# Moving small products, loads and waits in a one-core encoder layer

## The chip, the cores and the metric

The kernel runs on one core of a Trainium2 chip. The metric is the device time of one execution in microseconds (us), the median over several runs. The engines named below are TensorE (PE, matmuls; PEld is its weight load), VectorE (DVE), ScalarE (ACT), GpSimd (POOL) and SyncE (SP). SP, ACT and POOL also issue DMAs, each from a queue of its own that is worked off in order.

## The reference, cut to what matters

One layer of an encoder with a residual stream `h` of 256 tokens by 2048 channels: a hybrid mixer (a gated linear recurrence and an RWKV7 recurrence), cross attention over 256 memory tokens, and a SwiGLU block. Each is followed by a layer norm.

```python
def step(S, inp):                       # RWKV7, 32 heads of 64
    r_t, w_t, k_t, v_t, kk_t, b_t = inp
    sa = jnp.einsum('bhvk,bhk->bhv', S, kk_t)
    S = S * w_t[:, :, None, :] - sa[..., None] * b_t[:, :, None, :] + v_t[..., None] * k_t[:, :, None, :]
    return S, jnp.einsum('bhvk,bhk->bhv', S, r_t)
...
o = group_norm(o) * gn_g + gn_b
o = o + jnp.sum(r_h * k_h * r_k, axis=-1, keepdims=True) * v_h      # the "bonus"
return o * g                                                       # g = sigmoid(g_lo) @ gB
...
s = jnp.einsum('bthd,bmhd->bhtm', q, k) * (XATTN_HEAD_DIM ** -0.5)  # 4 heads of 512
p = jax.nn.softmax(s, axis=-1)
o = jnp.einsum('bhtm,bmhd->bthd', p, v)
h = layer_norm(ALPHA * h + o @ wo)
ff = (jax.nn.silu(h @ wg) * (h @ wu)) @ wd
```

All values are float32. Every large product is made from a high and a low part of both factors.

## The kernel before, in words

**The main stream.** All weights flow through one stream. A weight tile (2048 by 128, 1 MB) comes in two halves of 512 KB. For each half, `split_half` loads `raw` (four buffers, issued by SP), casts it to the high part `wh` on ACT (L156) and subtracts to get the low part `wl` on DVE (L158), three buffers each. In the mixer, `wstat_half` then multiplies: eight matmuls of 512 columns (L169: `wh` times high and low part of the activations) and eight of 256 columns (L172: `wl` times the high part). In the later stages, `xstat` keeps the activations stationary: for each half unit and each of the two token halves (`tt`) six matmuls of 512 columns (L243, L244, L246). `xstat` can group units: it makes all units of a group for token half 0, then all of them for token half 1, and holds a group's weights in tiles that a function `room` gives.

**Deferred work.** Small products run beside the stream. `defer(n, fn)` files a function, and `passed(mm)`, called at the end of every half unit, counts it down. When it is due, its instructions are traced with an order edge: those for PE come behind that matmul `mm`. Only PE is bound by this edge. The order on each engine is otherwise fixed when the program is built, by a planner that takes instructions by priority once they are ready by its own estimate of times. Instructions of the stream carry low priority numbers by their unit, all others count up in the order of tracing. On the chip each engine runs its fixed list in order and waits where data are late.

**The RWKV part.** Sixteen channel tiles form four groups. For each tile, `tile_stage` multiplies key, receptance and value columns (six halves) and defers: `key_direction` (normalized keys, L572 is its matmul), `receptance` (`rkf`, L603), `values` (two transposes L608 copied to `sv` on ACT at L610 and L611, and the bonus product L613 that DVE turns into `yb` at L614), `key_rows` (four transposes L619, copied to `bkt` on ACT at L620) and `products` (L627, masked into `gt` on DVE at L631). The PSUM tiles of all these come from one pool, `mix`, of three banks. `sq`, `rkf` and a group's later `on` share one SBUF buffer (tag A).

Three halves after a group's last tile, `recurrence` starts a triangular solve: SP writes parts of `gt` to DRAM and reads them back as `al`, DVE runs 31 dependent steps (L674, L677), SP writes the result out (L680) and reads it back as `ymat` (L685). PACE halves later `chunk_steps` is traced: DVE transposes `ymat` into `xz` (L692), PE starts with L697 and L707, and four chunks of matmuls follow (L726 to L756), then a group norm. At its end, for each of four tiles, come two transposes (L783), the norm's scale on ACT (L785), the bonus (L786), two products with gate weights `lwg` (L790) loaded on POOL's queue (L457), and the gate (L791). The next group's small work needs buffers that `chunk_steps` still reads, so most of it runs once `chunk_steps` is through. `decay_rates` for the next group loads `lw` and makes L518.

**Attention.** For each of four heads come four tiles of q (eight halves), the scores (L990 to L992), the softmax (L994 to L1001), the transposes of the weights (L1006) and the products with the values (L1014 to L1016) into `oT`. Then `wo` runs in four column blocks. Between blocks, DVE applies the scale and shift of the layer norm before (L1040, L1041) with row broadcasts `gb1` that POOL loads (L1025). The last block has its eight half units in two groups, whose split weights lie in the buffers of the values (`vh0`, `vh1`, `vl0`, `vl1`) and of `B`. Then the first half units of the gate matrix are split ahead into tiles `wsp` (L207, L208), and the second layer norm runs per token half (L926, L328, transposes L336, L338 to L346), queued on ACT and DVE behind these splits.

Of the kernel before, what the change touches and what calls it, by code (L numbers as in the profile page):

```python
# [18 lines left out]
P = 128  # L19
T = 256  # L20
# [7 lines left out]
NT = 16  # L28
NG = 4
DR = (7, 10)  # L30
PACE = (20, 28, 20, 20)
NB0, NB1 = 4, 7
ALPHA = float(2.0 ** 0.25)
LN_EPS = 1e-5
# [11 lines left out]
def trunk(ctx, tc, x, memT, vec, rows, consts, lruw, loraw, w_in, w_out, wq, wk, wv, wo, wgu, wd, out,  # L46
# [31 lines left out]
    def defer(n, fn):  # L78
        waiting.append([n, fn])
# [302 lines left out]
    with ExitStack() as mx:  # L382
# [72 lines left out]
        def small_load(dst, src):  # L455
            with tc.issue_after(front[-1]):
                nc.gpsimd.dma_start(dst, src)  # L457
# [49 lines left out]
        def decay_rates(g, jp, rates):  # L507

            if jp == 0:
                rates.append(grp.tile([P, 4, T], F32, name="avg"))  # L510
                rates.append(grp.tile([P, 4, T], F32, name="evg"))
            avg, evg = rates
            lw = wk1.tile([P, 2, 2, P], F32, name="lw")
            small_load(lw, loraw[2 * g + jp, :, 0:2])
            for n, dst in ((0, evg), (1, avg)):
                ps = mps()
                for jj in range(2):
                    nc.tensor.matmul(ps[:, jj * T:(jj + 1) * T], lw[:, n, jj, :], lo[n], start=True, stop=True)  # L518
                nc.scalar.activation(dst[:, 2 * jp:2 * jp + 2], ps.rearrange("p (j t) -> p j t", j=2), AF.Sigmoid)
            for j in range(2 * jp, 2 * jp + 2):  # L520
                nc.vector.tensor_tensor_scan(evg[:, j], cmask, evg[:, j], 0.0, ALU.mult, ALU.add)
# [40 lines left out]
        def tile_stage(g, j, i, u, fs, av, ev, dt, kr, bkt, sv, yb, gt):  # L562
# [72 lines left out]
            for nm, n in (("k", 1), ("r", 0), ("v", 2)):  # L635
# [4 lines left out]
                    defer(2, key_direction)  # L640
                elif nm == "r":
                    defer(1, receptance)
            defer(1, values)
            defer(2, key_rows)
            defer(3 if j == 3 else 4, products)

        def recurrence(g, kkr, gt, bkt, sv, dm, yb, scr, scx, pace):

# [38 lines left out]
            defer(pace, partial(chunk_steps, g, kkr, gt, bkt, sv, dm, yb, gi))  # L687

        def chunk_steps(g, kkr, gt, bkt, sv, dm, yb, gi):
            for pr in range(2):  # L690
                q = 64 * (1 - pr)
                nc.vector.transpose(xz[q:q + 32], ymat[q:q + 32, :, 0:32])  # L692
# [67 lines left out]
            for a in range(2):  # L760
# [12 lines left out]
                nc.vector.reciprocal(rv, vr)  # L773
                nc.vector.tensor_tensor(o3, o3, rv.rearrange("p (h o) -> p h o", o=1).broadcast_to([P, 8, 64]),
                                        ALU.mult)
            for j in range(4):
                i = 4 * g + j
                fs = slice(j * P, (j + 1) * P)
                lw = wk1.tile([P, 2, P], F32, name="lwg", bufs=2)
                small_load(lw, loraw[i // 2, :, 2:4, i % 2])  # L780
                ps = rps()
                for a in range(2):
                    last = nc.tensor.transpose(ps[:, a * P:(a + 1) * P], ot[a][:, fs], ident)  # L783
                on = wk1.tile([P, T], F32, name="on", tag="A")
                nc.scalar.activation(on, ps[:, 0:T], AF.Identity, scale=col("gn_g", i), bias=col("gn_b", i))  # L785
                nc.vector.tensor_tensor(on, on, yb[:, j, :], ALU.add)  # L786
                ps = rps()
                with tc.issue_after(last.ins):
                    for a in range(2):
                        nc.tensor.matmul(ps[:, 0:T], lw[:, a, :], lo[2 + a], start=(a == 0), stop=(a == 1))  # L790
                nc.vector.tensor_tensor(yb[:, j, :], on, ps[:, 0:T], ALU.mult)  # L791
            dump(f"yb{g}", yb)

        evac = [None]
# [138 lines left out]
    with at:  # L933
# [40 lines left out]
        for hd in range(XH):  # L974
            b0 = 4 * (hd % 2)
            qs = [pair(ap1, "q", f"B{b0 + k}") for k in range(4)]
            qh, ql = [h for h, _ in qs], [l for _, l in qs]
            for k in range(4):
                a = wtile(wq[hd * 4 + k], xTh, xTl)
                split_to(a, qh[k], ql[k])  # L980
            pp = [pair(ap1, "pT", f"B{8 + b0 // 2 + m}") for m in range(2)]
            pTh, pTl = [h for h, _ in pp], [l for _, l in pp]
            pn = []
            for tt in range(2):
                ts = slice(tt * P, (tt + 1) * P)
                ps = mp.tile([P, 512], F32, name="mix", tag="mix")
                s = ps[:, 0:NMEM]
                for k in range(4):
                    kk = hd * 4 + k
                    nc.tensor.matmul(s, qh[k][:, ts], kTh[kk], start=(k == 0), stop=False)  # L990
                    nc.tensor.matmul(s, qh[k][:, ts], kTl[kk], start=False, stop=False)
                    nc.tensor.matmul(s, ql[k][:, ts], kTh[kk], start=False, stop=(k == 3))  # L992
                mxx = sm_.tile([P, 1], F32, name="mxx")
                nc.vector.tensor_reduce(mxx, s, AX.X, ALU.max)  # L994
                pe = ap1.tile([P, NMEM], F32, name="pe", tag=f"B{12 + b0 // 2 + tt}")
                nc.vector.tensor_scalar(pe, s, mxx, None, ALU.subtract)
                sme = sm_.tile([P, 1], F32, name="sme")
                last = nc.scalar.activation(pe, pe, AF.Exp, scale=sc, accum_out=sme)
                rse = sm_.tile([P, 1], F32, name="rse")
                nc.vector.reciprocal(rse, sme)  # L1000
                nc.vector.tensor_scalar(pe, pe, rse, None, ALU.mult)  # L1001
                pn.append(pe)
            for m in range(2):
                ps = mp.tile([P, 512], F32, name="mix", tag="mix")
                for tt in range(2):
                    nc.tensor.transpose(ps[:, tt * P:(tt + 1) * P], pn[tt][:, m * P:(m + 1) * P], ident)  # L1006
                split_to(ps[:, 0:T], pTh[m], pTl[m])
            for k in range(4):
                kk = hd * 4 + k
                cs = slice(kk * P, (kk + 1) * P)  # L1010
                ps = mp.tile([P, 512], F32, name="mix", tag="mix")
                o = ps[:, 0:T]
                for m in range(2):
                    nc.tensor.matmul(o, vh[m][:, cs], pTh[m], start=(m == 0), stop=False)  # L1014
                    nc.tensor.matmul(o, vh[m][:, cs], pTl[m], start=False, stop=False)
                    nc.tensor.matmul(o, vl[m][:, cs], pTh[m], start=False, stop=(m == 1))  # L1016
                oTh[kk], oTl[kk] = pair(ap1, "oT", f"A{kk}")
                split_to(o, oTh[kk], oTl[kk])
        with tc.issue_after(last.ins):
            load_sqrt(sm_)  # L1020
        gb1 = []
# [11 lines left out]
            return [t[:, n * 512:(n + 1) * 512] for n in range(4)]  # L1033

        for nb in range(4):
            pt = xstat([wo[nb, u] for u in range(4)], oTh, oTl, [(4, room), (4, lambda i: room(i + 4))] if nb == 3 else None)
            for m in range(2 * nb, min(2 * nb + 2, 4)):
                for tt in range(2):
                    s = hres[:, tt, m * 512:(m + 1) * 512]
                    nc.vector.tensor_tensor(s, s, gb1[m], ALU.mult)  # L1040
                    nc.vector.tensor_tensor(s, s, gb1[4 + m], ALU.add)  # L1041
            if nb < 3:
                residual(nb, pt, st)
# [194 lines left out]
```

## Time and profile before

| | |
|---|---|
| three runs, median (lowest to highest) | 2109.88 us (2102.26 to 2113.18) |
| profiled execution, its own time | 2105.15 us |
| its span, first to last instruction | 2103.4 us |
| PE busy | 2067.1 us (98%) |
| DVE busy | 1389.2 us (66%) |
| ACT busy | 1097.6 us (52%) |
| mean granted PE clock | 0.993 |

The span and the times inside it come from the one profiled execution. Busy time of PE is modelled from pipelined matmuls, so "busy" can hide a slower pace. A row of the timeline gives start, duration, engine, line, operation, output and inputs, how often, and in brackets the idle time of that engine before it with what ended it.

### The profile page before, as it was taken

The page shows a single profiled execution, that of the slowest core. Times are in us where ns is not written, and L with a number is a line of the kernel's source. Part 1 is how long each engine was busy: PE and PEld are TensorE (multiplying, and loading weights), DVE is VectorE, ACT ScalarE, POOL GpSimd, SP SyncE. Part 2 cuts the span into 40 slices and gives each one's busy share as a digit, 9 for nine tenths or more (in the row PEclk, how much of TensorE's full clock was granted, in tenths as well). Part 3 has the DMA queues.
Part 4 walks back from the last instruction along what each step waited for, and adds up shares of the span by engine and source line. Part 5 has one row for each costly group of instructions (what it writes and reads, how often), then busy time and mean ns, then how long its engine had stood idle before and what let it go on. Part 6 is the DMA issues. An engine that isn't in the chain of part 4 may idle for free.

```text
span 2103.4 us, 30286 instructions
## 1 busy us (share of the span) xinstructions
PE 2067.1 (98%) x11588; PEld 1749.3 (83%) x11588; DVE 1389.2 (66%) x2157; ACT 1097.6 (52%) x1588; POOL 113.5 (5%) x176
## 2 busy tenths in 40 slices
PE   9999999999999999999999999999999999999997
PEld 8888888888888888888888888778888888888886
DVE  7787868968795986686755666645555544444455
ACT  6756755665564575665644444544444444433332
POOL 2100020020002000300000000000000000000000
PEclk9999999999999999999999999999999999999999
DMA  9645635644553465477555455655555555555554
GB/s 327 200 157 180 201 104 161 202 147 145 178 187 116 141 196 179 150 266 239 183 191 197 141 180 175 219 186 190 190 190 190 191 186 193 190 187 195 191 196 143
DMA packets 135761, 388.18 MB, mean 185 GB/s; under 512 B 38368, under 2 KB 42976, under 8 KB 134848
## 3 DMA queue, kind: packets, MB, share of 16 engines
q1 hardware_dynamic: 126368, 358.71, 52.4%
q0 software_dynamic: 6000, 19.27, 2.8%
q10 hardware_dynamic: 3248, 8.26, 1.1%
q8 instruction: 91, 1.49, 0.3%
q14 instruction: 54, 0.44, 0.1%
HBM read 375.31 MB, written 10.88 MB: 184 GB/s over the span
## 4 chain that ended last, share of the span: by engine, by line
PE 62%; DVE 4%; DMA 2%; issue 1%; ACT 1%; POOL 0%; DVEq 0%; SPq 0%; POOLq 0%; ACTq 0%
PE acc L244 15%; PE acc L243 15%; PE acc L246 15%; PE acc L169 7%; PE acc L172 4%; DVE wl L158 1%; DMA kr<-k_d 1%; DMA gb<-in_rows_dram 0%; PE mix L1092 0%; PE rec L731 0%; PE rec L738 0%; PE rec L756 0%; DVE pd L674 0%; DVE xi L677 0%; DMA lwg<-in_loraw_dram 0%
## 5 line engine op out<-in xcount | busy, mean ns | idle before, releaser
L158 DVE TENSOR_TENSOR wl<-raw,wh 128x1024 fp32r<-128x1024 f32 x640 | 782.1, 1223 | 564.9 <-ACT wh L156 522.1
L156 ACT CAST wh<-raw 128x1024 fp32r<-128x1024 f32 x640 | 670.6, 1050 | 673.5 <-PE acc L244 495.2
L169 PE MATMUL acc<-xT,wh 128*128 128x512 f32 x2112 | 556.1, 401 | 0.0
L169 PEld LDWEIGHTS acc<-xT,wh 128*128 128x128 f32 x2112 | 381.3, 190 | 69.0
L172 PEld LDWEIGHTS acc<-xT,wl 128*128 128x128 f32 x2112 | 290.6, 190 | 22.0
L172 PE MATMUL acc<-xT,wl 128*128 128x256 f32 x2112 | 305.6, 285 | 0.0
L243 PE MATMUL acc<-wh,xT 128*128 128x512 f32 x688 | 268.8, 391 | 0.0
L244 PE MATMUL acc<-wh,xT 128*128 128x512 f32 x688 | 267.8, 389 | 0.0
L246 PE MATMUL acc<-wl,xT 128*128 128x512 f32 x688 | 211.9, 389 | 0.4 <-DVE wl L158 0.4
L246 PEld LDWEIGHTS acc<-wl,xT 128*128 128x128 f32 x688 | 129.1, 188 | 27.8 <-DVE wl L158 0.8
L243 PEld LDWEIGHTS acc<-wh,xT 128*128 128x128 f32 x688 | 129.2, 188 | 26.7 <-ACT wh L156 0.2
L244 PEld LDWEIGHTS acc<-wh,xT 128*128 128x128 f32 x688 | 129.2, 188 | 26.5
L243 PE MATMUL acc<-wh,fh 128*128 128x512 f32 x336 | 130.8, 389 | 0.0
L244 PE MATMUL acc<-wh,fl 128*128 128x512 f32 x336 | 130.7, 389 | 0.0
L246 PE MATMUL acc<-wl,fh 128*128 128x512 f32 x336 | 103.5, 389 | 0.0
L246 PEld LDWEIGHTS acc<-wl,fh 128*128 128x128 f32 x336 | 63.1, 188 | 13.2
L243 PEld LDWEIGHTS acc<-wh,fh 128*128 128x128 f32 x336 | 63.1, 188 | 13.0
L244 PEld LDWEIGHTS acc<-wh,fl 128*128 128x128 f32 x336 | 63.1, 188 | 13.0
L191 ACT COPY jl<-acc 128x256 f32<-128x256 f32 x148 | 54.4, 367 | 11.3 <-PE acc L172 10.4
L194 DVE TENSOR_TENSOR js<-acc,jl 128x256 f32<-128x256 f32 x125 | 51.9, 415 | 1.3 <-ACT jl L191 1.2
L244 PE MATMUL acc<-wh,B 128*128 128x512 f32 x128 | 49.8, 389 | 0.0
L244 PE MATMUL acc<-wh,A 128*128 128x512 f32 x128 | 49.8, 389 | 0.0
(312 smaller groups left out, 2488.8 us busy)
## 6 DMA issues: line engine op xcount, KB each, us to landing
raw<-in_w_in_dram SPq DMA_DIRECT2D x232, 512.0 KB, 3.8
raw<-in_wgu_dram SPq DMA_DIRECT2D x176, 512.0 KB, 3.6
raw<-in_wd_dram SPq DMA_DIRECT2D x88, 512.0 KB, 3.6
raw<-in_wk_dram SPq DMA_DIRECT2D x32, 512.0 KB, 4.2
raw<-in_w_out_dram SPq DMA_DIRECT2D x32, 512.0 KB, 4.4
raw<-in_wv_dram SPq DMA_DIRECT2D x32, 512.0 KB, 3.6
raw<-in_wq_dram SPq DMA_DIRECT2D x32, 512.0 KB, 3.6
raw<-in_wo_dram SPq DMA_DIRECT2D x32, 512.0 KB, 3.7
```

The lines of the kernel that those rows point to most:

```text
L156: nc.scalar.copy(h, raw)
L158: su = nc.vector.tensor_tensor(l, raw, h.bitcast(F32), ALU.subtract)
L169: nc.tensor.matmul(acc, w, both[id(xh[k])], start=(k == 0), stop=False)
L172: mm = nc.tensor.matmul(acc[:, 0:T], l[:, kk * P:(kk + 1) * P], xh[k], start=False, stop=(k == 15))
L191: nc.scalar.copy(t, a[:, T:2 * T])
L194: nc.vector.tensor_tensor(out, a[:, 0:T], t, ALU.add)
L243: nc.tensor.matmul(pt[tt], xh[k0 + kk][:, ts], ws[kk], start=(k0 + kk == 0), stop=False)
L244: nc.tensor.matmul(pt[tt], xl[k0 + kk][:, ts], ws[kk], start=False, stop=False)
L246: mm = nc.tensor.matmul(pt[tt], xh[k0 + kk][:, ts], ws[2 + kk], start=False, stop=((u, hf) == end and kk == 1))
```

## The change

- `PACE` goes from (20, 28, 20, 20) to (21, 28, 21, 22): in groups 0 and 2 `chunk_steps` is traced one half unit later, in group 3 two.
- The gate weights are loaded for two tiles at once, at the start of `chunk_steps`. The two loads have a buffer each, one of them that of `lw`. The tail works on pairs of tiles: four transposes into one bank, eight products into another, then two tiles' scale, bonus and gate.
- `values`, `key_rows` and `products` of a tile are traced one after the other, four halves after the value columns (three for a group's last tile). Before, they were traced after one, two, and four or three halves.
- In attention, everything behind the softmax of a head (L1006 to the end of the head) is deferred by two half units: into the next head's q tiles, and for the last head into the first column block of `wo`.
- The last column block of `wo` is grouped as three and five half units in place of four and four. The buffers are handed out in the same order.

```diff
-PACE = (20, 28, 20, 20)
+PACE = (21, 28, 21, 22)
...
-            lw = wk1.tile([P, 2, 2, P], F32, name="lw")
+            lw = wk1.tile([P, 2, 2, P], F32, name="lw", tag="lw")
...
-            defer(1, values)
-            defer(2, key_rows)
-            defer(3 if j == 3 else 4, products)
+            def small_products():
+                values()
+                key_rows()
+                products()
+
+            defer(3 if j == 3 else 4, small_products)
...
         def chunk_steps(g, kkr, gt, bkt, sv, dm, yb, gi):
+            lws = []
+            for jp in range(2):
+                lws.append(wk1.tile([P, 2, 2, P], F32, name="lwg", tag=("lwg", "lw")[jp]))
+                small_load(lws[jp], loraw[2 * g + jp, :, 2:4])
...
-            for j in range(4):
-                i = 4 * g + j
-                fs = slice(j * P, (j + 1) * P)
-                lw = wk1.tile([P, 2, P], F32, name="lwg", bufs=2)
-                small_load(lw, loraw[i // 2, :, 2:4, i % 2])
+            for jp in range(2):
+                lw = lws[jp]
                 ps = rps()
-                for a in range(2):
-                    last = nc.tensor.transpose(ps[:, a * P:(a + 1) * P], ot[a][:, fs], ident)
-                on = wk1.tile([P, T], F32, name="on", tag="A")
-                nc.scalar.activation(on, ps[:, 0:T], AF.Identity, scale=col("gn_g", i), bias=col("gn_b", i))
-                nc.vector.tensor_tensor(on, on, yb[:, j, :], ALU.add)
-                ps = rps()
+                for j in range(2 * jp, 2 * jp + 2):
+                    for a in range(2):
+                        last = nc.tensor.transpose(ps[:, (j % 2) * T + a * P:(j % 2) * T + (a + 1) * P],
+                                                   ot[a][:, j * P:(j + 1) * P], ident)
+                pg = rps()
                 with tc.issue_after(last.ins):
-                    for a in range(2):
-                        nc.tensor.matmul(ps[:, 0:T], lw[:, a, :], lo[2 + a], start=(a == 0), stop=(a == 1))
-                nc.vector.tensor_tensor(yb[:, j, :], on, ps[:, 0:T], ALU.mult)
+                    for j in range(2):
+                        for a in range(2):
+                            nc.tensor.matmul(pg[:, j * T:(j + 1) * T], lw[:, a, j, :], lo[2 + a],
+                                             start=(a == 0), stop=(a == 1))
+                for j in range(2 * jp, 2 * jp + 2):
+                    i = 4 * g + j
+                    js = slice((j % 2) * T, (j % 2 + 1) * T)
+                    on = wk1.tile([P, T], F32, name="on", tag="A")
+                    nc.scalar.activation(on, ps[:, js], AF.Identity, scale=col("gn_g", i), bias=col("gn_b", i))
+                    nc.vector.tensor_tensor(on, on, yb[:, j, :], ALU.add)
+                    nc.vector.tensor_tensor(yb[:, j, :], on, pg[:, js], ALU.mult)
...
-            for m in range(2):
-                ...
+            def values_out(hd, pn, pTh, pTl):
+                ...
+
+            defer(2, partial(values_out, hd, pn, pTh, pTl))
...
-            pt = xstat(..., [(4, room), (4, lambda i: room(i + 4))] if nb == 3 else None)
+            pt = xstat(..., [(3, room), (5, lambda i: room(i + 3))] if nb == 3 else None)
```

More of the change, by code (lines that the diff above doesn't have):

```diff
@@ L1002, in trunk @@
                 pn.append(pe)
-            for m in range(2):
[L1004 to L1012, printed above, removed]
-                for m in range(2):
[L1014 to L1018, printed above, removed]
+            def values_out(hd, pn, pTh, pTl):
+                for m in range(2):
+                    ps = mp.tile([P, 512], F32, name="mix", tag="mix")
+                    for tt in range(2):
+                        nc.tensor.transpose(ps[:, tt * P:(tt + 1) * P], pn[tt][:, m * P:(m + 1) * P], ident)
+                    split_to(ps[:, 0:T], pTh[m], pTl[m])
+                for k in range(4):
+                    kk = hd * 4 + k
+                    cs = slice(kk * P, (kk + 1) * P)
+                    ps = mp.tile([P, 512], F32, name="mix", tag="mix")
+                    o = ps[:, 0:T]
+                    for m in range(2):
+                        nc.tensor.matmul(o, vh[m][:, cs], pTh[m], start=(m == 0), stop=False)
+                        nc.tensor.matmul(o, vh[m][:, cs], pTl[m], start=False, stop=False)
+                        nc.tensor.matmul(o, vl[m][:, cs], pTh[m], start=False, stop=(m == 1))
+                    oTh[kk], oTl[kk] = pair(ap1, "oT", f"A{kk}")
+                    split_to(o, oTh[kk], oTl[kk])
+            defer(2, partial(values_out, hd, pn, pTh, pTl))
         with tc.issue_after(last.ins):
@@ L1035, in trunk @@
         for nb in range(4):
-            pt = xstat([wo[nb, u] for u in range(4)], oTh, oTl, [(4, room), (4, lambda i: room(i + 4))] if nb == 3 else None)
+            pt = xstat([wo[nb, u] for u in range(4)], oTh, oTl, [(3, room), (5, lambda i: room(i + 3))] if nb == 3 else None)
             for m in range(2 * nb, min(2 * nb + 2, 4)):
```

## The prediction

> **What bounds the kernel now.** I read the page first, then the waits of TensorE (PE), then the stretches around each long wait.
>
> ```profile
> span 2103.4 us, 30286 instructions
> PE 2067.1 (98%) x11588; PEld 1749.3 (83%) x11588; DVE 1389.2 (66%) x2157; ACT 1097.6 (52%) x1588; POOL 113.5 (5%) x176
> ```
>
> PE is busy for 2067.1 of 2103.4 us. The same products are made after the change, so only three things can be won: idle time of PE (36.3 us, which includes the start and the end), time lost at a lower clock, and time lost between streams of matmuls.
>
> ```profile
> PE rec L697 <- DVE xz L692: 6.4, 3, 3.0
> PE mix L1006 <- DVE pe L1001: 4.2, 2, 2.3
> PE rec L790 <- DMA lwg<-in_loraw_dram: 3.9, 4, 2.1
> ...
> PE mix L613 <- DVE rkf L603: 0.5, 1, 0.5
> ```
>
> The columns are total us, times and longest. The first three rows, 14.5 us together, are the places that the change touches: the first matmuls after the triangular solve (L697), the transposes of the attention weights (L1006), and the gate products of a group (L790). I then looked at the clock around the two longest waits and around two others; the columns that matter are the stretch, PE's busy time and, third from the right, PEclk.
>
> ```profile
> core 0: us, PE busy (x) PEld busy (x) DVE busy (x) ACT busy (x) POOL busy (x), PEclk, DMA share, GB/s
> ...
> 635.10:641.80 6.70, 6.70 (x87) 5.24 (x86) 2.32 (x4) 2.04 (x4) 0.00 (x0) 0.50 0.81 268
> ...
> 822.90:829.50 6.60, 6.47 (x75) 5.11 (x76) 2.34 (x4) 0.58 (x1) 0.00 (x0) 0.50 0.64 218
> ...
> 882.00:889.00 7.00, 6.93 (x37) 6.01 (x38) 2.95 (x6) 3.93 (x8) 5.37 (x10) 1.00 0.91 310
> ...
> 1230.30:1237.00 6.70, 6.70 (x43) 5.91 (x44) 6.70 (x13) 4.04 (x10) 0.00 (x0) 1.00 0.45 146
> ```
>
> The granted clock is 0.50 for some 6.7 us right behind the waits of group 2 and group 3. Behind the waits that end at 882 and at 1230 us it stays at 1.00.
>
> **Part by part: later solve products.** These are the four places where a group's chunk work begins; the last bracket is the idle time of PE before the row.
>
> ```profile
> 250.12 0.24 PE L697 MATMUL rec<-xz,gt 32*32 32x32 f32 x2 [1.33 <-DVE xz L692]
> ...
> 438.63 0.56 PE L697 MATMUL rec<-xz,gt 32*32 32x32 f32 x23
> ...
> 634.70 0.24 PE L697 MATMUL rec<-xz,gt 32*32 32x32 f32 x2 [2.11 <-DVE xz L692]
> ...
> 816.50 1.23 DVE L158 TENSOR_TENSOR wl<-raw,wh 128x1024 fp32r<-128x1024 f32 x1 [0.51 <-ACT wh L156]
> 817.98 1.22 DVE L158 TENSOR_TENSOR wl<-raw,wh 128x1024 fp32r<-128x1024 f32 x1
> 822.28 0.70 DVE L692 STREAM_TRANSPOSE xz<-ymat 32x512 f32<-32x512 f32 x1 [2.74 <-DMA ymat<-scx]
> 823.03 0.31 PE L697 MATMUL rec<-xz,gt 32*32 32x32 f32 x2 [2.96 <-DVE xz L692]
> ```
>
> Group 1, whose PACE of 28 stays, has no wait. The unit of PACE is a half weight tile, which takes 2.80 us (381.32 to 384.12 below). The change holds L697 back by one half in groups 0 and 2 and by two in group 3. The joined products (below) put 0.85 us of PE work ahead of a group's last products and so delay the solve by that much. Net cover: 2.80 - 0.85 = 1.95 us against 1.33 (gone), 1.95 against 2.11 and, behind it, the second transpose of 0.70 (I leave 0.5), 5.60 - 0.85 = 4.75 against 2.96 (gone). Gain 1.33 + 1.6 + 2.96 = 5.9; ends 0 and 6.4. The work that takes the place of the wait is the main stream, whose weights must be split by then: in group 3 the two subtractions that end by 819.2 are ahead of the transpose, enough for two halves. If they were not, DVE's own 2.74 us would reach PE as a late wl.
>
> **The clock.** Two stretches of 6.70 and 6.60 us at 0.50 lose 3.35 + 3.30 = 6.65 us. They begin as the waits of 2.11 and 2.96 end. Behind the waits of group 3's gates and of head 2 nothing follows, so the link is not strict. I take three quarters, 5.0; ends 0 and 6.65. The Trainium skill ("TensorE: Matmul & The Clock Gate", Part 1) gives the cold state as coming after at least one idle window of about 3.4 us. This trace differs: its longest wait is 2.96 us, yet 0.50 follows. By the page neither stretch would hang on these waits and this term would be 0; that is a rival below.
>
> **Paired gate loads.**
>
> ```profile
> 300.94 0.89 PE L790 MATMUL rec<-lo,lwg 128*128 128x256 f32 x3 [0.40 <-DMA lwg<-in_loraw_dram]
> ...
> 882.07 0.45 PE L790 MATMUL rec<-lo,lwg 128*128 128x256 f32 x1 [2.15 <-DMA lwg<-in_loraw_dram]
> ...
> lw<-in_loraw_dram POOLq DMA_DIRECT2D x8, 256.0 KB, 3.9
> lwg<-in_loraw_dram POOLq DMA_DIRECT2D x16, 128.0 KB, 2.9
> ```
>
> Sixteen loads of 128 KB become eight of 256 KB, the size that the lw row shows at 3.9 us, issued at the start of the chunk work, some 50 us before that use (250.12 to 300.94 in group 0). Before, the third load of a group waited for a buffer. One pair now shares lw's buffer; its last reader, the decay products, comes long before. All 3.9 us go (end: 2.9, if the second evictions hold a bank). On POOL's queue the loads now stand ahead of the chunk's dms work, not between the gates.
>
> **Held-back value products.**
>
> ```profile
> 1228.80 0.69 DVE L1040 TENSOR_TENSOR hres<-hres,gb 128x512 f32<-128x512 f32 x1 [2.56 <-DMA gb<-in_rows_dram]
> 1230.26 0.44 PE L1006 MATMUL mix<-ct,pe 128*128 128x128 f32 x2 [2.27 <-DVE pe L1001]
> ...
> 1261.24 0.44 PE L1006 MATMUL mix<-ct,pe 128*128 128x128 f32 x2 [1.91 <-DVE pe L1001]
> ```
>
> The cause sits on DVE: it waits 2.56 us for a row broadcast from memory, and the softmax queues behind. That stays. But L1006 now comes two halves (5.6 us) later, so its 4.2 us are covered; end: 2, if the stalled DVE starves wl instead. For the last head the products move into the first tiles of wo, whose fourth unit needs them three halves on.
>
> **Joined small products.** One steady tile of group 0, and one half of the main stream with a small block behind it:
>
> ```profile
> 161.21 0.41 PE L608 MATMUL mix<-ct,zv 128*128 128x128 f32 x2
> ...
> 161.70 2.18 PE L169 MATMUL acc<-xT,wh 128*128 128x512 f32 x8
> ...
> 164.66 0.60 PE L619 MATMUL mix<-ct,bk 128*128 128x128 f32 x4
> 165.02 2.09 PE L169 MATMUL acc<-xT,wh 128*128 128x512 f32 x8
> ...
> 167.99 1.16 PE L627 MATMUL mix<-kkr,bk 64*128 64x128 f32 x16
> ```
> ```profile
> 381.32 2.00 PE L169 MATMUL acc<-xT,wh 128*128 128x512 f32 x8
> 383.17 1.11 PE L172 MATMUL acc<-xT,wl 128*128 128x256 f32 x8
> 384.12 1.03 PE L802 MATMUL mix<-uc,lrw 128*128 128x256 f32 x4
> 384.79 2.20 PE L169 MATMUL acc<-xT,wh 128*128 128x512 f32 x8
> 386.83 1.11 PE L172 MATMUL acc<-xT,wl 128*128 128x256 f32 x8
> ```
>
> From L169's start to L172's is 1.85 us in a clean half and 2.04 behind a small block: a switch costs 0.19 us. In a steady tile three blocks become one or two. About nine of sixteen tiles are steady; the others run in a rush once the chunk work of the group before lets go, and their order is set by data. 9 x 1.5 x 0.19 = 2.5 us saved; at most 3.4. Against it: six claims on three PSUM banks now follow each other (L608, L613, L619, two of L627, and L572 of the next tile).
>
> ```profile
> 162.03 0.37 ACT L611 COPY sv<-mix 64x256 f32<-64x256 f32 x1
> ```
>
> The second of the two copies that empty the first bank ends at 162.40, 1.19 us after L608 starts, PE reaches L627 after 0.49 (L608 and L613) + 0.36 (L619) = 0.85: 0.34 of waiting per tile, 3.1 in nine; with a weight cast in front of the copies (mean 1050 ns, row below) 1.4 per tile, 12.6. I take the former, since the planner can put main work between: net +0.6; ends -3.4 and +10.
>
> ```profile
> L156 ACT CAST wh<-raw 128x1024 fp32r<-128x1024 f32 x640 | 670.6, 1050 | 673.5 <-PE acc L244 495.2 <-PE acc L169 94.7 <-issue 55.4
> ```
>
> **3+5.**
>
> ```profile
> 1343.62 0.69 DVE L926 SCALAR_TENSOR_TENSOR hres<-hres,acc 128x512 f32<-128x512 f32 x1 [2.19 <-PE acc L246]
> ...
> 1346.02 1.00 DVE L328 TENSOR_SCALAR hres<-hres,mv,rs 128x512 f32<-128x512 f32 x2
> ...
> 1348.86 0.49 PE L336 MATMUL lnt<-ct,hres 128*128 128x128 f32 x3
> ```
>
> The first token half of the last product ends one unit's half earlier (2.80/2 = 1.4 us). But L336 starts when the second half ends, with its input ready 1.8 us before (1347.02), so earlier brings 0; at best 1.4. The fourth room, vl1, is now freed only in the second half, and by the order of the pools one of the gate's prefetched tiles lies over it, with this layer norm queued behind its casts. That eats the same slack: +0.3; end +2.3 (a cast of 1.05 and a subtraction of 1.22 one after the other).
>
> **Sum**, against the profiled execution's 2105.15 us: -5.9 - 5.0 - 3.9 - 4.2 + 0.6 + 0.3 = -18.1, 2087.1 us. The three runs shown have a median of 2109.88, 4.7 above that execution; I add half of it, since part of such a spread may be more half-clock stretches that then go too: **2089.5 us**, own range 2080 to 2098.
>
> **Rivals.** (1) The wait moves. The place of the transposes on DVE follows the planner's idea of the landing and not PACE, and the landing is late (2.74 us above). Then DVE's stall starves wl, PE stands as long as before and the clock still falls: only loads and values are won, 2105.15 - 8.1 + 0.9 + 2.4 = 2100.4. Against it: the two splits in hand in group 3, and group 1.
> (2) The half-clock stretches are not tied to these waits: 2089.5 + 5.0 = 2094.5. For it: 882 and 1230. Against: both stretches start within 0.5 us of the end of the two longest waits.
> (3) Slower: the joined products stand on their three banks. If each claim queues behind a cast on ACT and a subtraction on DVE in all sixteen tiles, some 2.5 us each, 40 us come back: 2105.15 - 13.1 + 40 + 2.4 = 2134.5. From 13.1/16 = 0.8 us a tile the gain is gone, from 1.6 it is slower by over 0.5%. For it: L608 and L613 have waited already (0.5 us above); against: the planner spreads such work.
>
> **Numbers.** About 0.5% (10.5 us) is what a measurement here can tell from no change, so faster means below 2099.3. Forecast 0.52 (0.50 faster, 0.02 same), rival 1 0.22 (0.06 and 0.16), rival 2 0.12 (0.10 and 0.02), rival 3 0.14 (0.02 same, 0.12 slower). Faster 0.66, same 0.22, slower 0.12. The range 2079 to 2112 takes in rivals 1 and 2 and some of the joined products' upper bound.
>
> **What would show it.** Right: the first three rows of PE's waits nearly gone; clock 1.00 through the starts of the chunk work; L608, L613, L619 and L627 in a row. Wrong: L169 or L172 waiting for wh or wl there; L627 or L572 waiting for ACT or DVE; L336 starting later behind the last wo product; 0.50 in other places.

## The result and the profile after

The changed kernel is slower: its median is 2119.76 us (2114.06 to 2122.33, 10 runs), that of the kernel before in the same session 2107.81 us (10 runs). The ratio is 1.0056 with a 95% interval of [1.0044, 1.0067], so 0.56% or 12 us lost where 18 to 20 us were to be won.

In the code after the change the lines have moved: the solve products are L704 (L697 before) behind the DVE transposes L699 (L692), the attention transposes L1018 (L1006) behind L1012 (L1001), the gate products L794 (L790), the row-broadcast affine L1054 (L1040). The small products keep L608 to L627.

Two lines of the page of the changed kernel, its span and its busy times:

```profile
span 2118.3 us, 30248 instructions
...
PE 2078.8 (98%) x11588; PEld 1758.7 (83%) x11588; DVE 1392.4 (66%) x2157; ACT 1098.4 (52%) x1590; POOL 108.8 (5%) x168
```

PE has the same 11588 matmuls, and is busy 11.7 us longer than before (2067.1), while its idle time grew by 3.2 (2118.3 - 2078.8 = 39.5 against 36.3). Most of the loss lies inside work. The waits of PE in the changed kernel (total us, times, longest):

```profile
PE rec L704 <- DVE xz L699: 8.8, 3, 4.0
PE mix L1018 <- DVE pe L1012: 4.0, 2, 2.1
PE acc L246 <- DVE wl L158: 2.2, 2, 1.8
...
PE acc L243 <- ACT wh L156: 0.9, 1, 0.9
```

Of the three waits that were to go, only that for the gate weights (3.9 us) is gone. The wait for the solve grew from 6.4 to 8.8 us, that for the softmax stayed (4.2 and 4.0). Of the rows behind weight splits, L246 grew from 0.4 to 2.2 us, and L243 behind `wh` is new.

**Where the busy time went.** The timeline of the changed kernel around the small products of the second tile of group 0, on ACT, PE and PE's weight loads:

```profile
130.07 0.38 PE L608 MATMUL mix<-ct,zv 128*128 128x128 f32 x2
...
130.72 0.60 PE L619 MATMUL mix<-ct,bk 128*128 128x128 f32 x4
130.95 0.37 ACT L611 COPY sv<-mix 64x256 f32<-64x256 f32 x1
131.34 0.51 ACT L570 ACTIVATE sq<-zk,vt 128x256 f32<-128x256 f32 x1
131.37 2.30 PE L627 MATMUL mix<-kkr,bk 64*128 64x128 f32 x16
131.88 0.59 ACT L620 COPY bkt<-mix 128x512 f32<-128x512 f32 x1
```
```profile
131.37 0.96 PEld L627 LDWEIGHTS mix<-kkr,bk 64*128 64x128 f32 x8 [0.28 <-ACT sv L611]
132.51 0.96 PEld L627 LDWEIGHTS mix<-kkr,bk 64*128 64x128 f32 x8 [0.18 <-ACT bkt L620]
```

And the same tile in the kernel before:

```profile
131.09 1.16 PE L627 MATMUL mix<-kkr,bk 64*128 64x128 f32 x16
```

The block of sixteen records takes 2.30 us in place of 1.16. L627 multiplies with array rows 0 to 63 into one bank and with rows 64 to 127 into another. Before, the two halves take turns, and in the records the two of a pair start within 0.01 us of each other. In the changed kernel all of the first half goes ahead, waits 0.28 us for the bank that L611 empties, and the second half starts at 132.51, after L620 (131.88 + 0.59 = 132.47) has emptied its bank; on ACT, L570 stands ahead of L620. PE's fixed order already has it so, which fits a planner that expects the second bank to come free later than the first and issues the first half alone. The fourth tile agrees about the bank: there L620 ends 0.56 us behind the start of the block, the second half begins at 0.61, and from the first to the last start it takes 1.49 us. From the first to the last start a block takes 0.89 us in all sixteen tiles before (14.24 us together); after, 2.03 us in five tiles, 2.40 in two, 1.49 in one and 0.89 in the other eight (23.56 together): 9.3 us more. In the two of 2.40 one product of the main stream stands between the halves, so 0.37 us of each is work and not loss:

```profile
360.38 1.16 PE L627 MATMUL mix<-kkr,bk 64*128 64x128 f32 x8
361.46 0.50 PE L169 MATMUL acc<-xT,wh 128*128 128x512 f32 x1
361.89 1.16 PE L627 MATMUL mix<-kkr,bk 64*128 64x128 f32 x8
```

The period of a tile in group 0 shows it: L627 starts 19.84 us apart before (111.25, 131.09), 20.83 after (110.54, 131.37).

**The solve.** Three rows of the changed kernel's timeline where chunk work begins in groups 0, 2 and 3:

```profile
254.81 0.31 PE L704 MATMUL rec<-xz,gt 32*32 32x32 f32 x2 [3.08 <-DVE xz L699]
...
646.14 0.24 PE L704 MATMUL rec<-xz,gt 32*32 32x32 f32 x2 [1.76 <-DVE xz L699]
...
839.40 0.31 PE L704 MATMUL rec<-xz,gt 32*32 32x32 f32 x2 [3.95 <-DVE xz L699]
```

Before, these waits were 1.33, 2.11 and 2.96 us. Counting the main stream's sixteen products per half unit that stand ahead of it, the solve stands behind 74.9, 125.0, 177.9 and 226.9 halves before, and behind 74.9, 125.0, 177.8 and 227.9 after. In groups 0 and 2 it was not moved at all. Nor does the triangular solve before it start later there: by the same count its first step on DVE stands behind 54.2 and 159.1 halves after, 54.6 and 159.5 before. In group 0 it takes longer, 64.0 us from the first step to the transposes against 60.7, and in group 3 it starts 2.2 halves later (206.1 against 203.9).

**The clock** in the same places (PEclk is the third number from the right):

```profile
254.10:260.80 6.70, 5.99 (x73) 4.73 (x74) 5.38 (x10) 1.87 (x4) 0.00 (x0) 0.50 0.72 228
646.60:653.30 6.70, 6.70 (x85) 5.08 (x85) 2.27 (x4) 2.04 (x4) 0.00 (x0) 0.50 0.67 231
837.80:844.50 6.70, 5.10 (x17) 4.27 (x18) 3.51 (x6) 2.68 (x6) 0.00 (x0) 0.50 0.71 241
```

The two stretches at 0.50 are still there, and a third came behind the longer wait of group 0, 10.24 us long in the clock records. Such time counts as busy: 30.7 us at half clock ahead of 2000 us, where before it was 20.5, make 5.1 us of the 11.7. The same figure is 23.9, 27.3 and 34.1 us in one execution each of three kernels below that leave PE's order in the mixer as it was (three and five, PACE and held-back values alone), so this part cannot be put down to the change.

**Attention.** The wait moved from the first pair of transposes to the second; DVE's own stall before it is as it was:

```profile
1243.74 0.69 DVE L1054 TENSOR_TENSOR hres<-hres,gb 128x512 f32<-128x512 f32 x1 [2.08 <-DMA gb<-in_rows_dram]
...
1247.87 0.44 PE L1018 MATMUL mix<-ct,pe 128*128 128x128 f32 x2 [1.91 <-DVE pe L1012]
```

**A new loss** lies at the border of the mixer and its output weights, 3.7 us in PE's progress:

```profile
967.16 0.41 ACT L253 CAST B<-mraw 128x256 fp32r<-128x256 f32 x1 [4.62 <-DMA mraw<-in_memT_dram]
...
969.79 0.50 PE L243 MATMUL acc<-wh,A 128*128 128x512 f32 x1 [0.90 <-ACT wh L156]
...
975.91 0.72 PE L246 MATMUL acc<-wl,A 128*128 128x512 f32 x2 [1.83 <-DVE wl L158]
```

ACT stands 4.62 us for a part of the memory tokens, the weight cast queues behind it, and the split comes late. Compared by the start of the same main product, the changed kernel is 3 us behind at the end of group 0's tiles, 9 after group 0's chunk start and gates, 12 at the end of group 2's tiles and 15 at the end of the mixer; nothing is added in the rest (this compares two profiled executions, 2103.4 and 2118.3 us). So in this execution some 7 us are lost among the tiles where L627 stands, 6 at the chunk start of group 0 (1.75 us more of waiting and the stretch of 10.24 us at half clock) and 4 at the border, and some 2 are won in other places.

### The profile page after: what moved, and what is told of

Its sections match the earlier page's. It is cut to its first block, busy times and chain, and to the rows that moved or that the text cites. A ratio compares the mean times of both kernels' runs of the same rounds, so it can differ in the third digit from the quotient of the medians.

```text
span 2118.3 us, 30248 instructions
## 1 busy us (share of the span) xinstructions
PE 2078.8 (98%) x11588; PEld 1758.7 (83%) x11588; DVE 1392.4 (66%) x2157; ACT 1098.4 (52%) x1590; POOL 108.8 (5%) x168
## 3 DMA queue, kind: packets, MB, share of 16 engines
q8 instruction: 91, 1.49, 0.3%
## 4 chain that ended last, share of the span: by engine, by line
PE 61%; DVE 5%; issue 1%; DMA 1%; ACT 1%; POOL 0%; DVEq 0%; ACTq 0%; SPq 0%; POOLq 0%
PE acc L244 15%; PE acc L246 15%; PE acc L243 15%; PE acc L169 8%; PE acc L172 4%; DVE wl L158 2%; PE mix L1106 0%; PE rec L738 0%; PE rec L763 0%; PE rec L745 0%; DVE pd L677 0%; PE rec L794 0%; DMA mraw<-in_memT_dram 0%; DVE xi L680 0%; ACT wh L156 0%
## 5 line engine op out<-in xcount | busy, mean ns | idle before, releaser
L172 PEld LDWEIGHTS acc<-xT,wl 128*128 128x128 f32 x2112 | 291.3, 191 | 22.3
L172 PE MATMUL acc<-xT,wl 128*128 128x256 f32 x2112 | 304.5, 285 | 0.0
L243 PE MATMUL acc<-wh,xT 128*128 128x512 f32 x688 | 268.6, 390 | 0.0
L246 PE MATMUL acc<-wl,xT 128*128 128x512 f32 x688 | 212.1, 389 | 0.4 <-DVE wl L158 0.4
L246 PEld LDWEIGHTS acc<-wl,xT 128*128 128x128 f32 x688 | 129.1, 188 | 27.7 <-DVE wl L158 0.8
L243 PEld LDWEIGHTS acc<-wh,xT 128*128 128x128 f32 x688 | 129.1, 188 | 26.6 <-ACT wh L156 0.2
L243 PE MATMUL acc<-wh,fh 128*128 128x512 f32 x336 | 130.8, 389 | 0.0
L246 PE MATMUL acc<-wl,fh 128*128 128x512 f32 x336 | 103.4, 389 | 0.0
L243 PEld LDWEIGHTS acc<-wh,fh 128*128 128x128 f32 x336 | 63.0, 188 | 13.1
L246 PEld LDWEIGHTS acc<-wl,fh 128*128 128x128 f32 x336 | 63.1, 188 | 13.1
L191 ACT COPY jl<-acc 128x256 f32<-128x256 f32 x148 | 54.2, 366 | 17.9 <-PE acc L172 17.1
L243 PE MATMUL acc<-wh,A 128*128 128x512 f32 x128 | 50.1, 391 | 1.0 <-ACT wh L156 0.9
L244 PE MATMUL acc<-wh,A 128*128 128x512 f32 x128 | 49.9, 390 | 0.0
```

Of the source, the lines that this page charges most:

```text
L172: mm = nc.tensor.matmul(acc[:, 0:T], l[:, kk * P:(kk + 1) * P], xh[k], start=False, stop=(k == 15))
L191: nc.scalar.copy(t, a[:, T:2 * T])
L243: nc.tensor.matmul(pt[tt], xh[k0 + kk][:, ts], ws[kk], start=(k0 + kk == 0), stop=False)
L244: nc.tensor.matmul(pt[tt], xl[k0 + kk][:, ts], ws[kk], start=False, stop=False)
L246: mm = nc.tensor.matmul(pt[tt], xh[k0 + kk][:, ts], ws[2 + kk], start=False, stop=((u, hf) == end and kk == 1))
```

## The experiments

Each kernel was timed against the kernel before in the same session. Theory A: the joined products cost the time, because the two row halves of L627 stop overlapping. Against it stand the moved solve, and waiting for banks as such. The other runs take the remaining edits one by one.

**Joined products undone in the changed kernel.**

```diff
-            defer(3 if j == 3 else 4, small_products)
+            defer(1, values)
+            defer(2, key_rows)
+            defer(3 if j == 3 else 4, products)
```

> The changed kernel with values, key rows and products deferred separately again; all else of the change stays. Theory A: the serial products (8.7 us) and the later start of the solve (2 to 5 us with its half-clock stretch) go, some 2.7 us of saved switches come back: about 2119.8 - 11 = 2109, with the gate loads' 3.9 us kept. Rival: the joined products are not the cause and another part is: 2117 or more.

Measured: 2103.68 us, ratio 0.9972 [0.9959, 0.9984]. The other four edits together are a gain of 0.28%; joining turns it into a loss of 0.56%, some 17.7 us. All blocks of L627 are back at 0.89 us but one (1.63). The waits for the solve fall to what they were or less, and the rows behind late weight splits are back at 0.4 us:

```profile
PE rec L701 <- DVE xz L696: 5.5, 3, 2.2
PE mix L1015 <- DVE pe L1009: 4.8, 3, 2.2
```

By the two profiled executions: 8.6 us in the blocks of L627 (23.56 - 14.98), 3.3 in the wait for the solve (8.8 - 5.5), 2.7 in the late splits (2.2 + 0.9 against 0.4), and 3.4 at the clock (30.7 us at half clock ahead of 2000 us against 23.9, half of the difference), 18.0 together, against 16.1 between the spans; what joining saves is not in this sum.

**Joined products alone in the kernel before.**

```diff
-            defer(1, values)
-            defer(2, key_rows)
-            defer(3 if j == 3 else 4, products)
+            def small_products():
+                ...
+            defer(3 if j == 3 else 4, small_products)
```

> The kernel before with only the joined small products. Theory A: the mirror image, +8.7 for serial halves, -2.7 for switches, +2 to 7 for a later solve: 2116 to 2121 against 2107.8. My prediction's price for this part was +0.6 (bounds -3.4 to +10): 2108.

Measured: 2120.09 us, ratio 1.0054 [1.0037, 1.0071]: 11.4 us, as much as the whole change. The blocks sum to 25.43 us, 11.2 more than before, while the wait for the solve does not grow (5.4 us). By the start of the same main products it falls behind by 3.3, 2.2, 3.4 and 0.9 us among the tiles of the four groups, 9.8 of the 11.8 us between the two spans. So the joined products lose by themselves, where the blocks of L627 stand.

**Turns forced in the changed kernel.**

```diff
+                prev = None
...
-                        nc.tensor.matmul(pt[hh][:, c * P:(c + 1) * P], ...)
+                        with ExitStack() as ex:
+                            if prev is not None:
+                                ex.enter_context(tc.issue_after(prev.ins))
+                            prev = nc.tensor.matmul(pt[hh][:, c * P:(c + 1) * P], ...)
```

> The changed kernel with one thing added: the eight L627 products of a tile are put in a fixed order, so that the two head halves (array rows 0 to 63 and 64 to 127) alternate, as they did before the change. Theory A (in seven tiles the two halves, which overlapped before, now run one after the other: 2.03 to 2.40 us per tile instead of 0.89): those tiles go back to about 0.9 us each, and the time falls by 8 to 9 us, less a switch or two per tile for a first product that stands alone: 2119.8 to about 2112. Theory B (the loss is waiting for the three banks, not the order): the order changes nothing that counts, 2118 to 2121.

Measured: 2115.06 us, ratio 1.0026 [1.0011, 1.0041]: some 6 us of the 12 come back. The pairs overlap again, but the planner now puts the first pair alone and three main products behind it (L627 is L631 here):

```profile
137.06 0.48 PE L631 MATMUL mix<-kkr,bk 64*128 64x128 f32 x2
137.47 0.96 PE L169 MATMUL acc<-xT,wh 128*128 128x512 f32 x3
138.36 1.16 PE L631 MATMUL mix<-kkr,bk 64*128 64x128 f32 x14
```

A steady tile of group 0 still loses 0.46 us against before, where the changed kernel lost 1.0. The order of the halves is about half of it.

**No turns in the kernel before.** This measures the disputed cost by itself: nothing is joined, but one half of the array goes ahead of the other.

```diff
-                for c in range(4):
-                    for hh in range(2):
+                for hh in range(2):
+                    for c in range(4):
```

> The kernel before with one edit: the sixteen products of a tile (L627) are issued as all eight of the first row half and then all eight of the second, in place of taking turns. Nothing is joined, moved or left out. Theory A (the price of the joined work is that the two halves of the array no longer overlap): each block takes 2.03 us from its first to its last start in place of 0.89, in sixteen tiles 1.14 x 16 = 18 us, so about 2127 us against 2109, ratio 1.008. Rival (the price of the joined work is waiting for banks and copies, as the prediction's third rival had it, and the order of the products is only a sign of it): the blocks may look longer, but PE had slack there, so within 4 us of the kernel before, ratio below 1.002.

Measured: 2113.31 us, ratio 1.0021 [1.0010, 1.0031], 4.4 us by the ratio. Neither was right. The block takes 1.71 us, not 2.30:

```profile
134.48 1.71 PE L627 MATMUL mix<-kkr,bk 64*128 64x128 f32 x16
```

Its records show why: here the first product of the second half starts ahead of the last of the first half, since both banks are free. So the 1.14 us of the changed kernel are two things: 0.55 us from the order (1.71 - 1.16), and 0.59 us more because the second half starts only when its bank has been emptied, and by then the first half has run out. Not all of the 0.55 reaches the tile's period: in group 0 it is 20.13 us (114.35 to 134.48) against 19.84, 0.28 more. The rest falls together with a wait of the kernel before. There `zv` (`z["v"]`, the values that L608 transposes) is ready at 161.05, while PE's weight loads have run out at 160.91, and some 0.25 us are lost:

```profile
160.58 0.47 DVE L492 SCALAR_TENSOR_TENSOR zv<-js,vt,zv 128x255 f32<-128x255 f32 x1
...
161.17 0.20 PEld L608 LDWEIGHTS mix<-ct,zv 128*128 128x128 f32 x2 [0.26 <-PE acc L172]
```

The row names L172, but without turns L608 begins before the last L172 has ended (145.04 against 145.21) and does not wait: PE comes later there, and `zv` is ready 0.11 us before L608's weight load. Where the rest of the 4.4 us lies, beyond 0.28 in each steady tile, was not settled.

**Transposes joined, products half a unit behind**, in the changed kernel:

```diff
-            defer(3 if j == 3 else 4, small_products)
+            def values_and_keys():
+                values()
+                key_rows()
+            defer(2 if j == 3 else 3, values_and_keys)
+            defer(3 if j == 3 else 4, products)
```

> The changed kernel with one edit: values and key_rows of a tile stay traced together, but one half unit earlier, so that products (L627) comes one half behind them, where it was. Theory A2 (what costs is that the products stand directly behind the transposes that still hold the banks, so that their second bank comes free late and the halves of the array run one after the other): the blocks fall back to 0.89 us in all steady tiles and the time to that of the kernel with the three apart, 2103 to 2105 against 2110, ratio 0.997. Rival (joining as such costs: three banks claimed in a row, or the later start of the solve): at most half of it comes back, 2112 or more, ratio above 1.001.

Measured: 2106.54 us, ratio 0.9995 [0.9982, 1.0008]: 12.9 of the 17.7 us come back. All blocks are at 0.89 us:

```profile
130.91 1.16 PE L627 MATMUL mix<-kkr,bk 64*128 64x128 f32 x16
...
150.47 1.16 PE L627 MATMUL mix<-kkr,bk 64*128 64x128 f32 x16
```

The period of a tile is 19.56 us, 0.28 less than the 19.84 before. Nearly all of this is the wait of 0.25 us for `zv`, which is ready long before L608 now; the switches themselves give 0.03. What is left to the kernel with all three apart is the wait for the solve of group 3 (4.5 us) and the border, where ACT stands 4.8 us for the memory tokens and PE again waits 1.8 for a split. The loss at the border goes with solve products of group 3 that stand at half 227.9, behind a solve that starts at 206.1 or later; the changed kernel, the one with turns forced, this one and the last one below have both, while with the products at 226.9 (before, all apart, loads with values) neither appears. No run moved this alone, so the link is not shown.

**PACE alone, in the kernel before.**

```diff
-PACE = (20, 28, 20, 20)
+PACE = (21, 28, 21, 22)
```

> The kernel before with PACE at (21, 28, 21, 22) and nothing else. Prediction's step: the waits of L697 in groups 0, 2 and 3 (6.4 us) nearly go and two half-clock stretches with them, -5.9 and -5.0, ratio 0.995. Theory now: in these groups the count of PACE has run out before the place that the planner gives the solve products by its own estimate, so the instructions stand in the same order as before and the row of L697 stays at 5 to 7 us: ratio 1.000 within 0.0015.

Measured: ratio 1.0007 [0.9995, 1.0020]. The instructions of all five engines stand in the order of before, the solve products behind the same 74.9, 125.0, 177.9 and 226.9 halves. PACE ends at half 70 in group 0, 174 in group 2 and 219 in group 3, so the planner's own estimate of the landing decides there. The row of waits, 6.4 us in the one execution of before and 4.5 here, with the same order, also shows how far it goes from one execution to the next:

```profile
PE rec L697 <- DVE xz L692: 4.5, 3, 2.1
```

**A PACE that binds, in the kernel before.** The first tile of groups 1 and 3 is deferred five halves longer, since its small work needs the buffers.

```diff
-PACE = (20, 28, 20, 20)
+PACE = (28, 28, 26, 20)
...
-                    defer(2, key_direction)
+                    defer(2 + ex, key_direction)      # ex = 5 for the first tile of groups 1 and 3
...
```

> The kernel before with PACE (28, 28, 26, 20), and the small work of the first tile in groups 1 and 3 deferred five halves longer so that the order stays possible. In the built order the solve products of group 0 now stand 2.06 halves later and those of group 2 1.1 halves later; with the change's PACE alone they stand where they were. If the waits of L697 are worth what they show: 1.33 and 2.11 us go and with the latter, where it occurs, a half-clock stretch of 3.4: 2107.8 to 2101 to 2104. Rival (the stall only moves to the weights): 2107 to 2109, with L169 or L172 waiting for wh or wl at 635 us.

Measured: ratio 1.0000 [0.9987, 1.0013]. The solve products of groups 0 and 2 now stand at half 77.0 and 179.0, and their waits (1.33 and 2.11 us) and the half-clock stretch behind the second are gone. In group 3, where nothing was moved, the wait is 1.3 us in this execution in place of 2.96, and no half clock follows it. But:

```profile
PE rec L792 <- DMA lwg<-in_loraw_dram: 6.5, 4, 2.7
...
PE rec L699 <- DVE xz L694: 1.9, 2, 1.3
```

The wait for gate weights grows by 2.6 us, with a half-clock stretch of 3.41 us behind two of them. Compared by main products, the kernel is 3.9 us behind the one before at half 176, ahead of group 2's solve products; it is 0.2 us in front at half 184, where both have done the same chunk work, and 1.6 behind from half 200 on; in group 0 it goes from 1.0 behind to 4.2. So group 2's gain of some 4 us is down to 2.3 within sixteen halves, and group 0 loses 3.2. Apart from the loads, what takes it back was not settled.

**Paired loads alone, in the kernel before** (the edit of the tail, the loads and the buffer, as in the change).

```diff
-                lw = wk1.tile([P, 2, P], F32, name="lwg", bufs=2)
-                small_load(lw, loraw[i // 2, :, 2:4, i % 2])
...
+                lws.append(wk1.tile([P, 2, 2, P], F32, name="lwg", tag=("lwg", "lw")[jp]))
+                small_load(lws[jp], loraw[2 * g + jp, :, 2:4])
```

> The kernel before with the paired gate loads alone. Prediction's step: the waits of the gate products for lwg, 3.9 us in four places, go: about 2105.5 against 2109.5, ratio 0.998. Rival: the gain is given back behind it, because the next group's small work and the weights then wait for something else: 2109 to 2110, ratio 1.000, with the row of lwg gone from PE's waits and another row larger by 2 to 4 us.

Measured: 2105.25 us, ratio 0.9984 [0.9969, 0.9999], 3.4 us by the ratio. No wait for lwg is left, and the first rows are the old ones:

```profile
PE rec L701 <- DVE xz L696: 6.2, 3, 2.3
PE mix L1014 <- DVE pe L1009: 3.6, 2, 1.8
```

**Held-back values alone, in the kernel before.**

```diff
+            defer(2, partial(values_out, hd, pn, pTh, pTl))
```

> The kernel before with the value products of attention held back by two half units, as in the change, and nothing else. Prediction's step: the wait of the transposes for pe (4.2 us) goes, ratio 0.998. Theory now: in the changed kernel all four transposes of a head are placed together with the second of the two softmax tiles, so the wait moves from the first pair to the second and stays at about 4 us: ratio 1.000, within 2 us, with a row of 3.5 to 5 us for the transposes behind pe.

Measured: ratio 0.9999 [0.9987, 1.0011]. The wait is still there, now in front of the second pair (2.2 us in each of two heads, and in one of them 1.1 us more in front of the first):

```profile
PE mix L1007 <- DVE pe L1001: 5.6, 3, 2.2
```

In the first head the first pair moves from half 321.25 to 322 and the second from 321.94 to 322: two halves of deferral bring the second pair 0.06 of a half, because the planner had already put it nearly there. In the last two heads, the ones that wait, the second pair does not move at all.

**Three and five alone, in the kernel before.**

```diff
-[(4, room), (4, lambda i: room(i + 4))]
+[(3, room), (5, lambda i: room(i + 3))]
```

> The kernel before with the last column block of wo grouped as three and five half units and nothing else. Prediction's step: +0.3 us, ends -1.4 and +2.3. Theory now, from the changed kernel's trace around that place: no effect, ratio 1.000 within 0.0007, with the start of the transposes L336 and the waits behind them as before.

Measured: ratio 1.0003 [0.9988, 1.0019]; no effect to be seen.

**Loads with values four halves back, in the kernel before.**

```diff
+            defer(4, partial(values_out, hd, pn, pTh, pTl))      # with the paired loads
```

> The kernel before with the paired gate loads and the value products held back by four half units in place of two; small products apart, PACE and the last column block as before. If the wait for pe is only a matter of distance: both the lwg wait (3.9 us) and the pe wait (4.2 us) go, 2101.5 against 2109.5, ratio 0.996. If DVE's stall for the row broadcast reaches PE as late wl instead: the pe row goes, a row of L169 or L172 behind wl takes its place, and only the loads are won: 2105.5, ratio 0.998.

Measured: 2100.91 us, ratio 0.9960 [0.9945, 0.9975]. By its median this is the fastest kernel of the case, and it meets the first of the two. The pairs of transposes (half 324 in the first head) wait for nothing; a smaller wait behind them, for the split of their result, takes part of it back:

```profile
PE rec L701 <- DVE xz L696: 4.7, 3, 2.1
PE mix L1024 <- DVE pT L254: 3.2, 2, 1.9
```

**The same with the PACE that binds** (that edit and the one before this together).

```diff
-PACE = (20, 28, 20, 20)
+PACE = (28, 28, 26, 20)
...
+            defer(4, partial(values_out, hd, pn, pTh, pTl))
```

> The kernel before with paired gate loads, value products held back by four halves, and solve products that really come later: PACE (28, 28, 26, 20) with the first tile of groups 1 and 3 deferred five halves longer. With the late solve alone the wait of L697 fell from 6.4 to 1.9 us and lwg's rose from 3.9 to 6.5; the paired loads take lwg's away. If lwg was what gave the gain back: 2.8 us more than loads and values alone (2100.9), about 2098, ratio 0.9945. Rival (the next group's small work, which comes later with the solve, gives it back): 2101 to 2103, ratio 0.996 to 0.997.

Measured: 2103.76 us, ratio 0.9978 [0.9965, 0.9990], not faster than without it. Groups 0 and 2 no longer wait, but the solve of group 3, whose PACE stays at 20 because its buffers are given up soon behind it, waits longer, and the border loss is there, so this run does not tell what the later solve of groups 0 and 2 is worth:

```profile
822.90 0.31 PE L703 MATMUL rec<-xz,gt 32*32 32x32 f32 x2 [4.26 <-DVE xz L698]
```

## Why the prediction was wrong, step by step

- **What bounds the kernel** held: PE, with the waits as listed. But the three ways to win that it named (idle time, clock, switches between streams) left out a fourth in which the change lost: how well PE's own work overlaps. Busy time rose by 11.7 us with the same matmuls.
- **"The change holds L697 back by one half in groups 0 and 2 and by two in group 3"** failed (-5.9, and with it the clock). PACE says when the work is traced, not where it stands. In group 0 it ends at half 70 while the products stand at 74.9, and the 20 of before ended at 69: that PACE did not bind could have been read from the order before. The sign was on record: rival 1 says that the place on DVE follows the planner's idea of the landing. Alone it measured 1.0007. The delay of the solve by 0.85 us, in the same step, did not come either: in groups 0 and 2 the solve starts 0.4 halves sooner.
- **The clock** (-5.0) fell with it, since the waits did not go. The link between wait and half clock holds in part: where a later solve took group 2's wait of 2.11 us away, its stretch went with it. But the step calls 2.11 and 2.96 the two longest waits, and its own rows have 2.27 and 2.15, both longer than 2.11, with no half clock behind them.
- **Paired loads** (-3.9) held: the wait is gone, and alone they measured -0.16%, 3.4 us.
- **Held-back values** (-4.2) failed in "L1006 now comes two halves (5.6 us) later": the second pair moved by 0.06 of a half or not at all. With four halves the step works and the row is gone, though 3.2 us of a new wait stand behind it.
- **Joined products** (+0.6, ends -3.4 and +10) is the step that turned the sign. Measured +11.4 us, just outside its upper end. The wait for the first bank was sized well (0.34 predicted, 0.28 in the row). That the saving came out as priced (0.28 us a tile won with transposes and bonus joined, 1.5 x 0.19 = 0.28) is luck: 0.25 of it is the wait for `zv`, which the step did not have. Missing was the second bank: the step counted six claims on three banks, but priced a wait for only the first of L627's two, and took its 1.16 us as fixed. The Trainium skill has both halves of the missing rule. "TensorE: Matmul & The Clock Gate", Part 3, says that matmuls in different row groups run concurrently; "TensorEngine Tiling (Array Packing)", Gotcha 1, that row tiles need different PSUM banks. The rows agree with the first: 1.16 us in turns, 1.71 one half behind the other, 2.30 with a wait between. No run puts two row halves into one bank.
- **3+5** (+0.3) held within its ends: no effect.
- **Rival 1** (2100.4) had the right mechanism for PACE, but took the values for won. **Rival 3** (2134.5) named the right place, three banks, and the right sign; it priced 2.5 us in all sixteen tiles where some 1.1 us in eight was lost (9.3 us in the blocks); the other eight blocks are as before.
- **The sum.** The edits measured alone add to 1.0047 (+0.54% joined, -0.16% loads, -0.01% values, +0.07% PACE, +0.03% three and five) against 1.0056 [1.0044, 1.0067] together. The difference is smaller than the intervals of the parts. The border loss shows only where edits meet; what it adds was not separated.

## What to carry to other kernels

Before work is put closer together, look for matmuls that run side by side in different rows of the array: they need all their banks free at the same moment, and a bank that comes free late makes them run one after the other, here in 2.30 us in place of 1.16. A count that says when work is traced moves nothing as long as the planner's estimate of its data stands later; read the place out of the instruction order before a gain is counted. And a wait that is really removed has to be followed to the next late thing: here the waits of 1.33 and 2.11 us went with a later solve, the wait for gate weights grew by 2.6, and the time stayed the same.

## What the runs showed of the hardware

The two row halves of the array overlap in part even when one is issued wholly ahead of the other, as long as neither waits: 1.71 us, between 1.16 in turns and 2.30 with a wait between.

The half clock follows idle time of PE, but not by a fixed length. Over the traces of all fourteen kernels, by the idle times of PE between 60 and 2000 us (as the rows' brackets give them, from modelled ends of matmuls), all eleven of 2.5 us or more had a stretch at 0.50 that began during the wait or up to 2.1 us behind it, 18 of 30 of 2.0 to 2.5 us, and 8 of 32 of 1.5 to 2.0 us. All other such stretches lie in the second layer norm, where several waits of about 1 us follow each other. The stretches last 3.41, 6.83 or 10.24 us, one to three times 3.41. The same wait can go either way: 2.11 us in group 2 of the kernel before was followed by 0.50, and in the fastest kernel, at the same place:

```profile
635.95 0.24 PE L701 MATMUL rec<-xz,gt 32*32 32x32 f32 x2 [2.12 <-DVE xz L696]
```
```profile
636.00:642.60 6.60, 6.60 (x156) 5.26 (x157) 2.67 (x4) 3.05 (x6) 0.00 (x0) 1.00 0.84 289
```

The Trainium skill ("TensorE: Matmul & The Clock Gate", Part 1) has the window as free-running and 3413 ns long, and the lengths agree. It has the cold state after at least one idle window; here less than one was enough: six of the eleven waits were of 2.66 to 3.19 us, so the measurement decides. That a wait has to cover most of one free-running window would explain the chances above, but no run tested it.
